# Hybrid attention layer on one core: the seven-product form in eight of the eleven down-projection blocks, the residual's turn in half parts, another order of the last additions

## The chip, the core and the metric

The kernel runs on one NeuronCore of a Trainium2 chip. Five engines work side by side, each through its own instructions in order: TensorE (PE: matmuls; PEld is its weight load), VectorE (DVE), ScalarE (ACT), GpSimd (POOL) and SyncE (SP), which here issues most DMAs. They wait for each other through semaphores. The metric is the device time of one execution in microseconds (us), the median of several runs; less is better. Before the change it is 385.23 us (three runs, 384.71 to 385.44).

## What is computed

One layer of a causal decoder on 256 tokens of width 1024, in float32: a norm, one input projection, two attention mixers with a gated merge, and then a gated feed-forward part with a short convolution, and a last norm. The change lies in the feed-forward part and the last norm:

```python
def conv_ffn(h, w_up, conv_w, conv_b, w_down):
    S = h.shape[1]
    u, gate = jnp.split(h @ w_up, 2, axis=-1)          # 2 x 2816 columns
    up = jnp.pad(u, ((0, 0), (CONV_WIDTH - 1, 0), (0, 0)))
    uc = conv_b
    for j in range(CONV_WIDTH):
        uc = uc + conv_w[j] * up[:, j:j + S]
    return (jax.nn.gelu(uc) * gate) @ w_down

# at the end of the layer
    x = x + conv_ffn(rmsnorm(x, g_ffn[l]), ...)
return rmsnorm(x, g_final)
```

## The kernel before

**Precision.** Every float32 operand of a large matmul is held as two parts, a high half (rounded to the PE's fast float32 form) and the rest (low half); a product is three matmuls: high x high, high x low, low x high. For each block of weights ACT writes the high half (`whi<-raw`, line 130) and DVE subtracts it from the raw weights (`wlo<-raw,whi`, line 134). Three buffers each exist for the raw weights, the high and the low halves. SP loads the raw weights, 1 MB a block (line 180), into a raw buffer whose split has ended.

**Units.** The kernel is a hand-written list of units, most with 1 MB of weights, and a loop over it (line 1211 on) that issues, for each unit, its matmuls, its evacuation, and the splits of the next units. The order of instructions on each engine is the order of that code. The feed-forward part has 11 blocks of 256 hidden columns. Block j has two units that multiply up (`mm_up`: first the convolved half, then the gate half, 48 matmuls of 128x256 each) and one that multiplies down, `downs[j]`, which stands two blocks later (`LAG` = 2).

**What DVE does for a block.** `ev_u` (lines 594 to 612) scales the first up-product out of PSUM (U), ACT and DVE make the convolution C, ACT its gelu; `ev_g` multiplies C with the second up-product (M); ACT copies M's high half (ah), and DVE writes its low half (al, line 642). Beside these stand the splits of the weights of later units, and in `turn` (line 1205) the turn of the residual: xT lies with the features in the partitions, and the end of the kernel needs X with the tokens there. DVE turns it in 32x256 pieces (STREAM_TRANSPOSE, line 1209), 32 in all, and after each of `downs[0]` to `downs[3]` stand eight of them.

**Eight or seven products.** A down-projection multiplies two halves of 128 hidden columns by 1024 output columns, for two groups of 128 tokens (t = 0, 1). The first 512 output columns (ch = 0) are done directly. For the other 512, `mm_down_part` makes eight products of 128x256, and `mm_sums` makes do with seven, after Strassen: it multiplies sums of the weights with sums of the activations and adds up in seven accumulators `ffn["P"]` in PSUM. With three matmuls a product a block has 48 matmuls directly and 24 + 21 = 45 with seven products. The sums cost work on DVE: `split_sums` makes sums of the weights (W, lines 171 to 173) and their halves (Wh on ACT, Wl on DVE, line 177), and `ev_g` three sums of M (lines 628 to 631), after which ah and al are 1024 wide and not 512. `split_sums` splits its block's weights two units ahead, and the direct blocks' are split one unit ahead. Blocks `FIRST_SUM` to 8 use seven products; before, FIRST_SUM is 4. The last two blocks (9 and 10) are direct.

**The end.** `downs[9]` and `downs[10]` are multiplied together, one output quarter after the other (`last`, line 1334), in the order (t, ch) = (0, 0), (0, 1), (1, 1), (1, 0). Ahead of it the results of the seven products are gathered: four subtractions into Q and five additions to X (`add`, line 1329). `last` adds a quarter to X, squares it (ACT), sums up the squares (POOL), multiplies with g_final into Y (POOL for the first tokens, DVE for the second), and `store` scales by the norm and writes the result. The quarters (0, 0) and (1, 1) lie in one PSUM tile (ps_s).

Of the kernel before, what the change touches and what calls it, by code (L numbers as in the profile page):

```python
# [15 lines left out]
OP = mybir.AluOpType  # L16
# [10 lines left out]
HALF = 1120  # L27
SHARED = {25: 1024, 26: 1024}
QUARTERS = ((0, 0, 512), (1, 0, 512), (0, 512, 256), (1, 512, 256), (1, 768, 256), (0, 768, 256))
FIRST_SUM = 4  # L30
EPS = 1e-6
BIG = 1e30
UW = 2240
# [62 lines left out]
def build(ctx, tc, a, out):  # L96
    nc = tc.nc
    V, A, P, T = nc.vector, nc.scalar, nc.gpsimd, nc.tensor
# [29 lines left out]
    def split_hi(u, c0=0, c1=None):  # L128
        c1 = c1 or u.n
        A.activation(u.hi[:, u.o + c0:u.o + c1], u.raw[:, c0:c1], AF.Copy)  # L130
# [9 lines left out]
    def hi_of(i):  # L140
        if 2 <= i < len(units):
            if units[i].load is not None:
                return
            split_tiles(units[i])
            split_hi(units[i], 0, 1792 if units[i] in downs[FIRST_SUM:NF - 2] else None)

    def lo_of(i):
        if 2 <= i < len(units):
# [7 lines left out]
            if i == NFIRST + 1:  # L156
                split_lo(units[i], 0, 1024)
                split_lo(units[i], 1024, 2048)
                return
            if units[i] in downs[FIRST_SUM:NF - 1]:  # L160
                return
# [431 lines left out]
    def ev_u(j):  # L593
        def f(u):
# [9 lines left out]

            if FIRST_SUM <= j - LAG:
                ffn.pop("sums")()
# [12 lines left out]
    def ev_g(j):  # L619
        def f(u):  # L620
# [4 lines left out]
            n = 4  # L625
            if FIRST_SUM <= j < NF - 2:
                n = 8
# [39 lines left out]
    def mm_sums(u, j):  # L667
# [4 lines left out]
        for q, x, k in ((2, 2, 1), (1, 0, 0), (3, 7, 2), (6, 6, 6), (5, 5, 4), (7, 4, 5), (4, 3, 7)):  # L672
            yh, yl = (wh[:, k], wl[:, k]) if k < 4 else (sh[:, k - 4], sl[:, k - 4])
            for n, (w, a_) in enumerate(((yh, h), (yh, l), (yl, h))):
                T.matmul(ffn["P"][q], a_[:, x], w, start=j == FIRST_SUM and n == 0 and q in (1, 5),  # L675
                         stop=j == NF - 3 and n == 2 and q in (1, 5, 6, 7), skip_group_check=True)
# [31 lines left out]
    downs = [Unit(2048, mm_down(j), o=48) for j in range(NF)]  # L708
# [452 lines left out]
    for n, f in zip(CHUNKS, first):  # L1161
        for c in range(0, 768 * n, 768):
            x, r = f[:, c:c + 256], [f[:, c + 256:c + 512], f[:, c + 512:c + 768]]
            if k == 0:
                r[1] = f[:, 520:776]
            h, h32, l = [[q[:, k * 256:k * 256 + 256] for q in t] for t in
                         ((u0.hi, u1.hi), (u0.hi.bitcast(F32), u1.hi.bitcast(F32)), (u0.lo, u1.lo))]
# [36 lines left out]

    def turn(n):

        b, t = n // 2, n % 2
        for j in range(4):
            V.transpose(X[32 * j:32 * j + 32, t].rearrange("p (k c) -> p k c", c=128)[:, :, 32 * b:32 * b + 32],  # L1209
                        xT[32 * b:32 * b + 32, :, t * 128 + 32 * j:t * 128 + 32 * j + 32])  # L1210

    post = []
    for i, u in enumerate(units):
        if i == FIRST_ITEM:
            rt["identr"] = att.tile([128, 128], F32R, name="identr")
            A.activation(rt["identr"], ident, AF.Copy)
        if i == 9:
            cmp_sum()
        for it in batches.get(i - 1, []):
            it.fin()  # L1220
        if i == FIRST_ITEM + 6:
            dil_tiles()
        for it in at(i):
            if isinstance(it, Dil):
                it.split()
        for it in at(i - 3):
            it.te()
        if i == 11:
            cmp_kv_ev()
        for it in at(i - 1):  # L1230
            it.sm()
        if i > 2 and i != 6:
            lo_of(i + 1)
        if i == 10:
            cmp_gelu()
        for it in at(i - 1):
            it.sm2()
        for it in at(i - 1):
            it.send("MA" if isinstance(it, Cmp) else {20: "KH", 21: "KL"}.get(i, "MB%d" % (i % 2)))
        load_to(i + LA)  # L1240
        if i == 14:
            nc.sync.dma_start(xT, a["xT"])
        if i == 3:
            hi_of(5)
            mixer_tiles()
            u1.evac(u1)
        if i == 4:
            split_keys()
        if i == 14:

            ob = att.tile([128, 4, S], F32R, name="ob", tag="qa")
            OB.update(h=ob[:, 0:2], l=ob[:, 2:4])
        if i in (23, 24):
            for c in range(2):
                m = ML[i - 23, c]
                A.activation(m, m, AF.Sigmoid)
        if i == NFIRST:
            st.close()
            ffn["pool"] = ctx.enter_context(tc.tile_pool(name="ffn", bufs=1))
            gf = ffn["pool"].tile([128, D], F32, name="gf")  # L1260
            nc.scalar.dma_start(gf, bass.AP(tensor=a["g_final"].tensor, offset=a["g_final"].offset,
                                            ap=[[0, 128], [1, D]]))
            X = ffn["pool"].tile([128, 2, D], F32, name="X")
            sq = ffn["pool"].tile([128, 512], F32, name="sq")
            Y = ffn["pool"].tile([128, 2, D], F32, name="Y")
        if 24 <= i <= 25:
            hi_of(i + 2)
        if i in (3, 24, NFIRST + 2):
            rt["kick"] = "own"
        u.mm(u)  # L1270
        if i == 2:
            split_tiles(units[3])
            for c in (0, 1024):
                split_hi(units[3], c, c + 1024)
        if not 24 <= i <= 26 and i > 1 and i != 3:
            hi_of(i + 2)
        if i == 5:
            lo_of(7)
        if units[min(i + 2, len(units) - 1)] in downs[FIRST_SUM:NF - 2]:
            split_sums(units[i + 2])  # L1280
        if units[min(i + 2, len(units) - 1)] is downs[NF - 2]:
            split_lo(units[i + 2])
        if i == 2:
            lo_of(3)
            row_scale()
            u0.evac(u0)
            ev_cmp2()
        if i == NFIRST + 1:
            rt["R2"] = rows_of(rt["rs2"], "R2", "o")
            units[NFIRST].evac(units[NFIRST])  # L1290
        if post:
            post.pop()()
        if u.pre:
            u.pre(u)
        if u.evac and i not in (0, 1, NFIRST):
            u.evac(u)
        if i == 4:
            tables_pool4()
        if i in (6, 7):
            q_parts(i - 6)  # L1300
        if i == 7:
            gates_of()
        if u in downs[:4]:
            for n in range(2):
                turn(2 * downs.index(u) + n)
        if u.pre:
            post.append(post_g(len([q for q in units[:i] if q.pre])))
        first = [it for it in at(i) if isinstance(it, Nsa) or isinstance(it, Dil) and it.t]
        for it in first:
            it.qk()  # L1310
        if i == 11:
            at(i)[-1].by_keys()
        for it in at(i - 2):
            it.tr()
        for it in at(i):
            if it not in first:
                it.qk()
        for it in batches.get(i, []):
            it.pv()
        if i == 9:  # L1320
            cmp_fold()
        if i == 10:
            cmp_kv()
# [4 lines left out]
    def add(xs, y, t):  # L1328
        V.scalar_tensor_tensor(xs, y, rt["rs2"][:, t:t + 1], xs, op0=OP.mult, op1=OP.add)

    def last(t, ch, c0=0, c1=512):

        xs, y = X[:, t, ch * 512 + c0:ch * 512 + c1], ffn["y"][t][ch][:, c0:c1]
        w = c1 - c0
        if c0:
            y = pd([512])[:, :w]
        for j in (NF - 2, NF - 1):
            mm_down_part(downs[j], j, [(t, ch)], c0, c1, y if c0 else None)
        n = {(0, 0): 0, (0, 1): 1, (1, 1): 2, (1, 0): 3}[t, ch] + (c0 > 0)
        ss, r = ss3[:, n:n + 1], rs3[:, t:t + 1]  # L1340
        add(xs, y, t)
        if c0:
            V.tensor_tensor_reduce(out=sq[:, w:2 * w], in0=xs, in1=xs, scale=1.0 / D, scalar=r,
                                   op0=OP.mult, op1=OP.add, accum_out=ss)
        else:
            A.activation(sq[:, :w], xs, AF.Square, scale=1.0 / 32, accum_out=ss)  # L1346
            P.tensor_tensor(out=r, in0=epsc if t == ch else r, in1=ss, op=OP.add)  # L1347
        if c0 or t < ch:
            P.tensor_tensor(out=r, in0=ss if c0 else r, in1=nhalf[:, 0:1], op=OP.pow)
        (V if t else P).tensor_tensor(out=Y[:, t, ch * 512 + c0:ch * 512 + c1], in0=xs,  # L1350
                                      in1=gf[:, ch * 512 + c0:ch * 512 + c1], op=OP.mult)

    def store(t, c):
# [8 lines left out]
    p, q = ffn["P"], ffn["pool"].tile([128, 4, 256], F32, name="Q", tag="W")  # L1362
    A.activation(q[:, 0], p[1], AF.Copy)
    add(X[:, 0, 512:768], p[1], 0)
    for o, l, r, op in ((1, p[6], q[:, 0], OP.subtract), (2, q[:, 1], p[5], OP.subtract),
                        (3, q[:, 2], p[7], OP.subtract), (0, p[7], q[:, 1], OP.subtract)):
        V.tensor_tensor(out=q[:, o], in0=l, in1=r, op=op)
    add(X[:, 0, 768:1024], q[:, 2], 0)
    add(X[:, 1, 768:1024], q[:, 3], 1)
    add(X[:, 1, 512:768], q[:, 0], 1)  # L1370
    add(X[:, 1, 256:512], ffn["y"][1][0][:, 256:512], 1)
    last(0, 0)
    last(0, 1)
    last(1, 1)
    last(1, 0, 0, 256)
# [23 lines left out]
```

## Time and profile before

| | |
|---|---|
| median of three runs | 385.23 us |
| the profiled execution | 385.59 us, of which its span is 383.8 us |
| granted TensorE clock | 0.999 of full speed |
| instructions in the trace | 8148 |
| the feed-forward part | from about 206 us on |
| PE's last matmul | ends at 377.7 us |
| DMA | 78.26 MB, 204 GB/s over the span |

The span is the time from the first to the last recorded instruction. The page gives the busy time of each engine; the view by stretches gives it for parts of the span; the view in order of time gives each instruction's start, its duration, its engine and line, what it writes and reads, and in brackets how long the engine had been idle before it and what ended that. PE's matmuls overlap, so the time that one of them takes in a row is longer than the distance to the next.

### The profile page before, as it was taken

How to read it: one execution, taken by the hardware profiler on the slowest of the kernel's cores; microseconds unless marked ns; L12 is line 12 of the kernel's file. 1: busy time of each engine (PE TensorE's matmuls, PEld its weight loads, DVE VectorE, ACT ScalarE, POOL GpSimd, SP SyncE). 2: the span in 40 equal slices, each digit the busy share in tenths (PEclk: the TensorE clock that was granted, in tenths of full speed). 3: DMA queues.
4: the chain of work that ended last, by engine and by line, in shares of the span. 5: the costliest groups of instructions: out<-in, count | busy, mean ns of one | idle time of the engine just before them, and what ended most of it. 6: DMA issues, size and time to landing. Idle time of an engine off the chain costs nothing.

```text
span 383.8 us, 8148 instructions
## 1 busy us (share of the span) xinstructions
PE 375.6 (98%) x3402; PEld 370.1 (96%) x3402; DVE 314.2 (82%) x543; ACT 221.7 (58%) x312; POOL 36.2 (9%) x63
## 2 busy tenths in 40 slices
PE   7999999999999999999999999999999999999993
PEld 6999999999999999999999999999999999999993
DVE  5969599994996876468887799798999999989774
ACT  4966536775985745745534765345462745755523
POOL 4021300001000000250333000000000000000013
PEclk9999999999999999999999999999999999999999
DMA  8999354468454656363547365365465475485002
GB/s 276 415 388 363 124 208 176 166 237 323 172 205 150 235 219 232 140 219 110 197 148 297 137 256 229 111 219 197 157 224 207 163 263 208 139 312 193 30 0 111
DMA packets 13717, 78.26 MB, mean 204 GB/s; under 512 B 1520, under 2 KB 2032, under 8 KB 6000
## 3 DMA queue, kind: packets, MB, share of 16 engines
q1 hardware_dynamic: 13248, 76.89, 54.4%
q10 hardware_dynamic: 432, 0.85, 0.6%
q8 instruction: 27, 0.44, 0.5%
q14 instruction: 10, 0.08, 0.1%
HBM read 71.05 MB, written 1.05 MB: 188 GB/s over the span
## 4 chain that ended last, share of the span: by engine, by line
PE 96%; DMA 2%; DVE 1%; ACT 0%; issue 0%; SPq 0%; POOLq 0%; POOL 0%; ACTq 0%
PE ps_d L205 36%; PE ps_d L210 18%; PE ps_s L661 6%; PE ps_t L661 5%; PE ps_o L205 5%; PE ps_d L308 3%; PE ps_o L210 3%; PE ps_d L365 2%; PE ps_t L205 2%; PE ps_o L675 2%; PE ps_t L908 2%; DMA first<-in_first_dram 2%; PE ps_o L977 1%; PE ps_o L563 1%; PE ps_o L1098 1%; PE ps_s L205 1%
## 5 line engine op out<-in xcount | busy, mean ns | idle before, releaser
L134 DVE TENSOR_TENSOR wlo<-raw,whi 128x2048 fp32r<-128x2048 f32 (+3 forms) x62 | 133.4, 2155 | 5.2 <-ACT whi L130 5.1
L130 ACT ACTIVATE whi<-raw 128x2048 fp32r<-128x2048 f32 (+3 forms) x62 | 113.7, 1839 | 10.7 <-DMA raw<-in_wts_dram 6.0
L205 PE MATMUL ps_d<-hTh,whi 128*128 128x256 f32 x512 | 119.0, 278 | 0.0
L205 PE MATMUL ps_d<-hTl,whi 128*128 128x256 f32 x512 | 117.9, 276 | 0.0
L205 PEld LDWEIGHTS ps_d<-hTh,whi 128*128 128x128 f32 x512 | 96.1, 188 | 0.9 <-issue 0.7
L205 PEld LDWEIGHTS ps_d<-hTl,whi 128*128 128x128 f32 x512 | 96.1, 188 | 0.0
L210 PE MATMUL ps_d<-hTh,wlo 128*128 128x256 f32 x512 | 63.3, 276 | 0.0
L210 PEld LDWEIGHTS ps_d<-hTh,wlo 128*128 128x128 f32 x512 | 60.5, 188 | 0.0
L602 ACT ACTIVATE C<-U,small 128x256 f32<-128x256 f32 x22 | 12.1, 595 | 27.1 <-DVE U L598 27.1
L610 DVE SCALAR_TENSOR_TENSOR C<-U,small,C 128x256 f32<-128x256 f32 x44 | 18.9, 479 | 4.1 <-ACT C L602 4.1
L633 ACT ACTIVATE ah<-M 128x512 fp32r<-128x512 f32 (+1 forms) x11 | 9.1, 829 | 22.6 <-DVE M L631 11.8
L945 ACT ACTIVATE E<-E,ast 128x256 f32<-128x256 f32 (+1 forms) x32 | 14.1, 450 | 9.6 <-DVE ast L940 7.7
L1347 POOL TENSOR_TENSOR tiny<-cst,tiny 128x1 f32<-128x1 f32 x2 | 0.5, 246 | 164.1 <-ACT sq L1346 164.1
L134 POOL TENSOR_TENSOR wlo<-raw,whi 128x1024 fp32r<-128x1024 f32 x3 | 7.8, 2600 | 71.3 <-ACT whi L130 71.3
L175 ACT ACTIVATE Wh<-W 128x1024 fp32r<-128x1024 f32 x5 | 5.3, 1065 | 15.8 <-DVE W L173 15.8
L1209 DVE STREAM_TRANSPOSE X<-xT 32x256 f32<-32x256 f32 x32 | 14.0, 436 | 0.4
L661 PE MATMUL ps_s<-whi,ah 128*128 128x256 f32 x68 | 11.8, 276 | 0.0
L661 PE MATMUL ps_s<-wlo,ah 128*128 128x256 f32 x68 | 11.8, 276 | 0.0
L661 PE MATMUL ps_s<-whi,al 128*128 128x256 f32 x68 | 11.8, 276 | 0.0
L205 PE MATMUL ps_d<-whi,hTh 128*128 128x256 f32 x48 | 11.3, 282 | 0.0
L623 DVE TENSOR_TENSOR M<-ps_d,C 128x512 f32<-128x512 f32 x10 | 6.9, 691 | 5.2 <-ACT C L616 3.0
L205 PE MATMUL ps_d<-whi,hTl 128*128 128x256 f32 x48 | 11.1, 277 | 0.0
(312 smaller groups left out, 773.7 us busy)
## 6 DMA issues: line engine op xcount, KB each, us to landing
raw<-in_wts_dram SPq DMA_DIRECT2D x59, 1024.0 KB, 4.8
Er<-E SPq DMA_DIRECT2D x6, 512.0 KB, 3.2
first<-in_first_dram SPq DMA_DIRECT2D x7, 384.0 KB, 7.2
Er<-E SPq DMA_DIRECT2D x6, 384.0 KB, 2.9
raw<-in_wts_dram SPq DMA_DIRECT2D x2, 560.0 KB, 9.3
xn<-in_xn_dram SPq DMA_DIRECT2D x2, 512.0 KB, 8.9
w1k<-in_wts_dram SPq DMA_DIRECT2D x2, 512.0 KB, 7.3
w1v<-in_wts_dram SPq DMA_DIRECT2D x2, 512.0 KB, 8.0
```

The source lines that it names most:

```text
L130: A.activation(u.hi[:, u.o + c0:u.o + c1], u.raw[:, c0:c1], AF.Copy)
L134: (eng or V).tensor_sub(u.lo[:, u.o + c0:u.o + c1], u.raw[:, c0:c1], u.hi.bitcast(F32)[:, u.o + c0:u.o + c1])
L205: T.matmul(po, l, r, start=start and bank not in banks, stop=False, skip_group_check=True)
L210: T.matmul(po, l, r, start=False, stop=stop and n == len(ks) - 1, skip_group_check=True)
L308: T.matmul(u.p[:, i], l[:, kt, i * 128:i * 128 + 128], r[:, kt], start=kt == 0 and i == 0 and q == 0, stop=kt == 7 and q == 2, skip_group_ ...
L365: T.matmul(u.p[:, i], l[:, kt, i * 128:i * 128 + 128], r[:, kt], start=kt == 0 and i == 0 and q == 0, stop=kt == 7 and q == 2, skip_group_ ...
L602: A.activation(C[:, c], U[:, c, 2:], AF.Identity, scale=CW(2, t), bias=CB[:, t:t + 1])
L610: V.scalar_tensor_tensor(C[:, c], U[:, c, w:w + S], CW(w, t), C[:, c], op0=OP.mult, op1=OP.add)
L633: A.activation(h[:, :n], M[:, :n], AF.Copy)
L661: T.matmul(ffn["y"][t][ch][:, b:b + 256] if own is None else own, x[:, 2 * kt + t], quarter(w, kt, ch, b), start=j == (0 if own is None el ...
L945: A.activation(self.E[:, i], self.E[:, i], AF.Exp, bias=mn[:, i:i + 1], scale=-1.0, accum_out=dn[:, i:i + 1])
L1209: V.transpose(X[32 * j:32 * j + 32, t].rearrange("p (k c) -> p k c", c=128)[:, :, 32 * b:32 * b + 32], xT[32 * b:32 * b + 32, :, t * 128 + ...
```

## The change

Three things change.

1. `FIRST_SUM` becomes 1: blocks 1 to 8 use seven products, and only blocks 0, 9 and 10 are direct.
2. `turn` does half a part (two pieces of 32x256), and `TURNS` lays the sixteen half parts after `downs[0]` to `downs[8]`: 4, 2, 2, 2, 2, 1, 1, 1, 1, which is 8, 4, 4, 4, 4, 2, 2, 2, 2 pieces. There are still 32 pieces.
3. At the end, `last(0, 0)` stands behind the first half of the gathering and not behind all of it, and the multiplication of (0, 1) with g_final moves from POOL to DVE.

```diff
-FIRST_SUM = 4
+FIRST_SUM = 1
+TURNS = (4, 2, 2, 2, 2, 1, 1, 1, 1)
...
     def turn(n):

-        b, t = n // 2, n % 2
-        for j in range(4):
+        b, t = n // 4, n % 4 // 2
+        for j in range(2 * (n % 2), 2 * (n % 2) + 2):
             V.transpose(X[32 * j:32 * j + 32, t].rearrange("p (k c) -> p k c", c=128)[:, :, 32 * b:32 * b + 32],
                         xT[32 * b:32 * b + 32, :, t * 128 + 32 * j:t * 128 + 32 * j + 32])
...
-        if u in downs[:4]:
-            for n in range(2):
-                turn(2 * downs.index(u) + n)
+        if u in downs[:len(TURNS)]:
+            n = downs.index(u)
+            for n in range(sum(TURNS[:n]), sum(TURNS[:n + 1])):
+                turn(n)
...
-        (V if t else P).tensor_tensor(out=Y[:, t, ch * 512 + c0:ch * 512 + c1], in0=xs,
+        (V if t or ch else P).tensor_tensor(out=Y[:, t, ch * 512 + c0:ch * 512 + c1], in0=xs,
                                       in1=gf[:, ch * 512 + c0:ch * 512 + c1], op=OP.mult)
...
     add(X[:, 0, 512:768], p[1], 0)
-    for o, l, r, op in ((1, p[6], q[:, 0], OP.subtract), (2, q[:, 1], p[5], OP.subtract),
-                        (3, q[:, 2], p[7], OP.subtract), (0, p[7], q[:, 1], OP.subtract)):
-        V.tensor_tensor(out=q[:, o], in0=l, in1=r, op=op)
+    V.tensor_sub(q[:, 1], p[6], q[:, 0])
+    V.tensor_sub(q[:, 2], q[:, 1], p[5])
     add(X[:, 0, 768:1024], q[:, 2], 0)
+    last(0, 0)
+    V.tensor_sub(q[:, 3], q[:, 2], p[7])
+    V.tensor_sub(q[:, 0], p[7], q[:, 1])
     add(X[:, 1, 768:1024], q[:, 3], 1)
     add(X[:, 1, 512:768], q[:, 0], 1)
     add(X[:, 1, 256:512], ffn["y"][1][0][:, 256:512], 1)
-    last(0, 0)
     last(0, 1)
```

What this does to DVE's order in a block is seen behind the turns that follow `downs[0]`. On DVE, before, from those turns (the first row) to the turns that follow `downs[1]`:

```order
L1209 STREAM_TRANSPOSE X<-xT 32x8x32 x8
L134 TENSOR_TENSOR wlo<-raw,whi 128x2048
L597 MEMSET U 128x2x2
L598 TENSOR_TENSOR U<-ps_d,R_2771 128x2x256
L610 SCALAR_TENSOR_TENSOR C<-U,small,C 128x256 x4
L134 TENSOR_TENSOR wlo<-raw,whi 128x2048
L623 TENSOR_TENSOR M<-ps_d,C 128x512
L134 TENSOR_TENSOR wlo<-raw,whi 128x2048
L642 TENSOR_TENSOR al<-M,ah 128x512
L1209 STREAM_TRANSPOSE X<-xT 32x8x32 x8
```

On DVE, after the change, from the same turns on (the rest of the block follows in the next piece):

```order
L1210 STREAM_TRANSPOSE X<-xT 32x8x32 x8
L135 TENSOR_TENSOR wlo<-raw,whi 128x2048
L172 TENSOR_TENSOR W<-raw 128x512
L173 TENSOR_TENSOR W<-W,raw 128x256
L174 TENSOR_TENSOR W<-W,raw 128x256
L135 TENSOR_TENSOR wlo<-raw,whi 128x1792
L598 MEMSET U 128x2x2
L599 TENSOR_TENSOR U<-ps_d,R_2771 128x2x256
L178 TENSOR_TENSOR Wl<-W,Wh 128x1024
L611 SCALAR_TENSOR_TENSOR C<-U,small,C 128x256 x4
```

The weights' sums and the split of `downs[1]` now stand ahead of U, and Wl behind it. The rest of that block on DVE, after the change:

```order
L624 TENSOR_TENSOR M<-ps_d,C 128x512
L629 TENSOR_TENSOR M<-M 128x256
L631 TENSOR_TENSOR M<-M 128x128
L632 TENSOR_TENSOR M<-M 128x128
L135 TENSOR_TENSOR wlo<-raw,whi 128x2048
L643 TENSOR_TENSOR al<-M,ah 128x1024
L1210 STREAM_TRANSPOSE X<-xT 32x8x32 x4
```

M has lost the split that stood between it and C, has got its three sums behind it, al is twice as wide, and half as many turns follow.

At the end of the kernel, on DVE, before, from the last split of weights to the addition of the quarter (0, 1) (ps_o, ps_t and ps_s are PSUM tiles; X<-ps_s is the quarter (0, 0)):

```order
L134 TENSOR_TENSOR wlo<-raw,whi 128x2048
L1329 SCALAR_TENSOR_TENSOR X<-ps_o,tiny,X 128x256
L1367 TENSOR_TENSOR Q<-ps_o,Q 128x256
L1367 TENSOR_TENSOR Q<-Q,ps_o 128x256 x2
L1367 TENSOR_TENSOR Q<-ps_o,Q 128x256
L1329 SCALAR_TENSOR_TENSOR X<-Q,tiny,X 128x256 x3
L1329 SCALAR_TENSOR_TENSOR X<-ps_t,tiny,X 128x256
L1329 SCALAR_TENSOR_TENSOR X<-ps_s,tiny,X 128x512
L1329 SCALAR_TENSOR_TENSOR X<-ps_t,tiny,X 128x512
```

The same place on DVE after the change:

```order
L1210 STREAM_TRANSPOSE X<-xT 32x8x32 x2
L135 TENSOR_TENSOR wlo<-raw,whi 128x2048
L1331 SCALAR_TENSOR_TENSOR X<-ps_o,tiny,X 128x256
L1367 TENSOR_TENSOR Q<-ps_o,Q 128x256
L1368 TENSOR_TENSOR Q<-Q,ps_o 128x256
L1331 SCALAR_TENSOR_TENSOR X<-Q,tiny,X 128x256
L1331 SCALAR_TENSOR_TENSOR X<-ps_s,tiny,X 128x512
L1371 TENSOR_TENSOR Q<-Q,ps_o 128x256
L1372 TENSOR_TENSOR Q<-ps_o,Q 128x256
L1331 SCALAR_TENSOR_TENSOR X<-Q,tiny,X 128x256 x2
L1331 SCALAR_TENSOR_TENSOR X<-ps_t,tiny,X 128x256
L1331 SCALAR_TENSOR_TENSOR X<-ps_t,tiny,X 128x512
```

Two turns stand ahead of the last split, and the addition X<-ps_s has moved ahead of two of the four subtractions and three of the additions.

## The prediction

> **What bounds the kernel now.** I read the page first, then the busy times by stretch, then VectorE's (DVE's) instructions in order of time. The page's busy shares and its chain of waits:
>
> ```profile
> PE 375.6 (98%) x3402; PEld 370.1 (96%) x3402; DVE 314.2 (82%) x543; ACT 221.7 (58%) x312; POOL 36.2 (9%) x63
> ...
> PE 96%; DMA 2%; DVE 1%; ACT 0%; issue 0%; SPq 0%; POOLq 0%; POOL 0%; ACTq 0%
> ```
>
> TensorE (PE) is the bound: the chain that ended last is 96% PE, and DVE has a fifth of the span free. But a share over the span says nothing of one stage. The feed-forward stage, by stretches (busy us of each engine, granted clock, DMA):
>
> ```profile
> 227.00:276.00 49.00, 49.00 (x435) 49.00 (x434) 43.04 (x61) 23.80 (x21) 0.00 (x0) 1.00 0.55 201
> ...
> 296.00:341.00 45.00, 45.00 (x400) 45.00 (x399) 42.16 (x57) 26.86 (x24) 0.00 (x0) 1.00 0.59 212
> ```
>
> The third number with a count is DVE. From 227 to 276 us (blocks with eight products) it is busy 43.04 of 49.00 us, 88%; from 296 to 341 us (blocks with seven) 42.16 of 45.00, 94%. PE is full in both. So a block with seven products fills DVE nearly as much as PE, and it does so in a stretch in which no turn of the residual stands. The change puts turns into exactly such blocks. What PE needs for one, from its own timeline (the low-half matmuls of an up-projection, one block apart, and the last block's):
>
> ```profile
> 306.29 1.98 PE L210 MATMUL ps_d<-hTh,wlo 128*128 128x256 f32 x16
> ...
> 322.27 1.98 PE L210 MATMUL ps_d<-hTh,wlo 128*128 128x256 f32 x16
> ...
> 368.85 0.62 PE L661 MATMUL ps_s<-wlo,ah 128*128 128x256 f32 x4
> ```
>
> Between the first two lie 48 + 48 + 45 = 141 matmuls in 15.98 us, 0.1133 us each. Nine matmuls fewer are 1.02 us.
>
> **What DVE needs for a block.** I count rounds, from one start of U<-ps_d (row L598) to the next. One round with eight turns and the step from eight to seven products, and one with seven products and no turns:
>
> ```profile
> 276.18 0.68 DVE L598 TENSOR_TENSOR U<-ps_d,R 128x512 f32<-128x512 f32 x1
> ...
> 281.52 0.69 DVE L623 TENSOR_TENSOR M<-ps_d,C 128x512 f32<-128x512 f32 x1
> ...
> 283.24 2.28 DVE L134 TENSOR_TENSOR wlo<-raw,whi 128x2048 fp32r<-128x2048 f32 x1
> 285.44 1.22 DVE L642 TENSOR_TENSOR al<-M,ah 128x1024 fp32r<-128x1024 f32 x1
> 286.67 3.61 DVE L1209 STREAM_TRANSPOSE X<-xT 32x256 f32<-32x256 f32 x8
> 290.31 2.29 DVE L134 TENSOR_TENSOR wlo<-raw,whi 128x2048 fp32r<-128x2048 f32 x1
> ...
> 295.99 0.68 DVE L598 TENSOR_TENSOR U<-ps_d,R 128x512 f32<-128x512 f32 x1
> ...
> 300.17 0.69 DVE L623 TENSOR_TENSOR M<-ps_d,C 128x512 f32<-128x512 f32 x1 [0.78 <-ACT C L616]
> ...
> 304.09 1.22 DVE L642 TENSOR_TENSOR al<-M,ah 128x1024 fp32r<-128x1024 f32 x1
> 305.23 2.28 DVE L134 TENSOR_TENSOR wlo<-raw,whi 128x2048 fp32r<-128x2048 f32 x1
> ...
> 310.90 0.68 DVE L598 TENSOR_TENSOR U<-ps_d,R 128x512 f32<-128x512 f32 x1
> ```
>
> - The round of the step takes 295.99 - 276.18 = 19.81 us, with no wait for PE in it.
> - A round of seven products without turns takes 310.90 - 295.99 = 14.91 us. The 0.78 us before M is inside: the split that used to stand there has moved away, so DVE waits for ScalarE's (ACT's) gelu. Against PE's 15.98 us DVE gains 1.07 us a round.
> - Turns: from al to the split behind them 290.31 - 285.44 = 4.87 us with eight, 305.23 - 304.09 = 1.14 us with none, so eight cost 3.73 us. Their busy time is 3.61 us, 0.45 each; I put the other 0.12 us down as fixed for a group. Groups of four and of two stand nowhere in the trace: four cost between 1.81 us (0.45 each, nothing fixed) and 2.28 (one more turn's time as the fixed part); I take 0.45 each + 0.12, 1.93 and 1.03 us, since it lies with the one group that the trace shows.
>
> So a round with four turns takes 14.91 + 1.93 = 16.84 us, **0.86 us more than PE needs**, and one with two 15.94 us, as long as PE's.
>
> **The sum.** The change makes blocks 1 to 3 (from 0) seven-product blocks and lays the turns as 8, 4, 4, 4, 4, 2, 2, 2, 2 behind blocks 0 to 8. I follow DVE from the first place that differs:
>
> ```profile
> 223.57 0.68 DVE L623 TENSOR_TENSOR M<-ps_o,C 128x512 f32<-128x512 f32 x1
> 224.17 2.27 DVE L134 TENSOR_TENSOR wlo<-raw,whi 128x2048 fp32r<-128x2048 f32 x1
> 226.37 0.68 DVE L642 TENSOR_TENSOR al<-M,ah 128x512 fp32r<-128x512 f32 x1
> ...
> 227.05 0.69 DVE L598 TENSOR_TENSOR U<-ps_d,R 128x512 f32<-128x512 f32 x1
> ...
> 243.37 0.69 DVE L598 TENSOR_TENSOR U<-ps_d,R 128x512 f32<-128x512 f32 x1 [1.49 <-PE ps_d L210]
> ```
>
> 1. Block 1's M gets its three sums: M to split 283.24 - 281.52 = 1.72 us in place of 224.17 - 223.57 = 0.60; al grows from 0.68 to 1.22. The next U moves from 227.05 to 227.05 + 1.12 + 0.54 = 228.71.
> 2. The round behind it is now the step, with eight turns: 228.71 + 19.81 = 248.52. Before, it ended at 243.37, and 1.49 us of it was waiting for PE; that wait is used up.
> 3. Four rounds with four turns: 4 x 16.84 = 67.36, to 315.88. Two with two turns: 31.88, to 347.76.
> 4. The last round, before:
>
> ```profile
> 340.70 0.68 DVE L598 TENSOR_TENSOR U<-ps_d,R 128x512 f32<-128x512 f32 x1
> ...
> 345.77 0.69 DVE L623 TENSOR_TENSOR M<-ps_d,C 128x512 f32<-128x512 f32 x1 [1.67 <-PE ps_d L210]
> ...
> 356.25 0.69 DVE L598 TENSOR_TENSOR U<-ps_d,R 128x512 f32<-128x512 f32 x1 [1.31 <-PE ps_d L210]
> ...
> 359.92 2.29 DVE L134 TENSOR_TENSOR wlo<-raw,whi 128x2048 fp32r<-128x2048 f32 x1 [0.26 <-ACT whi L130]
> ...
> 363.51 0.69 DVE L642 TENSOR_TENSOR al<-M,ah 128x512 fp32r<-128x512 f32 x1 [0.70 <-ACT ah L633]
> 365.32 2.29 DVE L134 TENSOR_TENSOR wlo<-raw,whi 128x2048 fp32r<-128x2048 f32 x1 [1.12 <-ACT whi L130]
> ```
>
> It took 15.55 us with two waits for PE: 1.31, and 1.67 of which 0.78 is the gelu and stays. Without them and with two turns: 15.55 - 1.31 - 0.89 + 1.03 = 14.38, to **362.14** in place of 356.25.
>
> 5. From that U to the end of the last split of weights (365.32 + 2.29 = 367.61) are 11.36 us, of splits and of hand-overs between DVE and ACT that all start from U. Block 8's two turns (0.93 us) fall into the 1.12 us wait in it; unhidden they would cost 0.93. The split now ends at 362.14 + 11.36 = 373.50. PE used it at 368.85, with 1.24 us in hand; now it starts some 0.03 us behind it, at 373.53: **4.68 us late**.
>
> PE's 1.02 us buys nothing here: it turns into new waits for DVE, some 0.9 us a block at the low-half matmuls of the first up-projection from about 290 us on, and over 2 us in the last two blocks. Behind such a wait on PE stand 16 matmuls, then the second up-projection's 48, whose result DVE's M needs: 64 x 0.1133 = 7.3 us after the split. DVE's next M comes 300.17 - (283.24 + 2.28) = 14.7 us after it, so DVE does not wait in turn, and the lateness does not feed on itself. ACT gets a copy (Wh) and a longer ah in each of the three blocks; in the stretch with seven products it is busy 26.86 of 45.00 us, so they lie beside DVE's work. SP's and ACT's issues of DMA keep their order.
>
> 6. The end. Rows of before (DVE, then PE's second tokens, DVE and POOL):
>
> ```profile
> 371.15 0.74 DVE L1329 SCALAR_TENSOR_TENSOR X<-ps_s,tiny,X 128x512 f32<-128x512 f32 x1
> ...
> 372.03 0.65 PE L661 MATMUL ps_s<-whi,ah 128*128 128x256 f32 x4
> ...
> 374.98 0.75 DVE L1329 SCALAR_TENSOR_TENSOR X<-ps_s,tiny,X 128x512 f32<-128x512 f32 x1 [2.00 <-PE ps_s L661]
> 375.03 1.30 POOL L1350 TENSOR_TENSOR Y<-X,gf 128x512 f32<-128x512 f32 x1
> ...
> 375.77 1.12 DVE L1350 TENSOR_TENSOR Y<-X,gf 128x512 f32<-128x512 f32 x1
> ...
> 378.02 0.19 POOL L1347 TENSOR_TENSOR tiny<-tiny 128x1 f32<-128x1 f32 x1 [1.09 <-ACT sq L1346]
> 378.33 0.48 DVE L1343 CUSTOM_DVE_ANT_0 sq<-X,tiny 128x256 f32<-128x256 f32 x1
> ```
>
> The addition of the first tokens (X<-ps_s) ended 371.89 - 367.61 = 4.28 us behind the last split; PE's second tokens write the same tile and come 372.03 - 368.85 = 3.2 us behind the split's use. In the old order a late split would cost another 1.1 us there. Drawn ahead of half of the gathering (two subtractions and three additions, some 1.9 us) it ends in time, so this part costs nothing and saves that 1.1. The product with gf that POOL gives up runs on DVE in the 2.00 us in which it waits for PE's next result; beside a gathering that is late by what the split is late, little of that wait is left, but a product of 0.7 to 1.1 us still ends about when that result comes. The other one, 1.12 us on DVE at 375.77, ran beside POOL's 1.30. The nearest row alone is the 128x512 sum in the same rounds:
>
> ```profile
> 292.52 0.69 DVE L171 TENSOR_TENSOR W<-raw 128x512 f32<-128x512 f32 x1
> ```
>
> If it falls to that, the square and POOL's sum behind it come 0.4 us sooner, and the last reduction starts at the end of the last addition, about 0.1 us earlier; otherwise nothing. I take 0.1. The Trainium skill, GPSIMD Engine Reference, section Specifications, says that GpSimd's SBUF interfaces are shared with VectorE and contend with DVE instructions with two SBUF inputs. By that rule the 0.1 us comes; without it, 0; the trace agrees so far as 1.12 beside 0.69 goes.
>
> Together 4.68 - 0.1 = **+4.6 us** against the profiled execution's 385.59 (span 383.8), 390.2. That execution lies 0.36 us above the median of 385.23; from the median it is **389.8**.
>
> **The rivals.**
> - *The work stays hidden, and PE sets the end* (the other side). Its place is DVE's idle time, 1.49 us in the first round and the like in the next, 0.89 + 1.31 in the last, and the 1.24 us at the end. The price is then -1.02 - 0.1: 384.5 profiled, **384.1**. For it: PE is full in both stretches, and DVE idles 18% of the span. It decides at the point where a round of DVE is shorter than 15.98 us; four turns in 14.91 go past that by 0.86. Only turns under 0.27 us each would bring it back. Chance 0.09. The Trainium skill, Perfetto Trace Analysis, section Identifying the Most-Contended Engine, tells one to take LDWEIGHTS busy as TensorE's measure and to improve the engine with the highest share first; by it (PEld 96%, DVE 82%) this rival is the forecast. The stretches agree on the order before the change, and do not on what is left over: 2.84 us of DVE in 45.
> - *The end catches up.* The hand-overs with ACT in step 5 (0.26 + 0.70 + 1.12 us idle on DVE) would be done already when DVE comes late. Against it: each starts from an instruction of DVE behind U. It gives 389.8 - 2.1 = **387.7**. Chance 0.12.
> - *Late splits make late loads.* A raw buffer is loaded anew when its split has ended:
>
> ```profile
> raw<-in_wts_dram SPq DMA_DIRECT2D x59, 1024.0 KB, 4.8
> ...
> raw<-in_wts_dram SPq DMA_DIRECT2D x2, 560.0 KB, 9.3
> ```
>
> A round of 16.8 us leaves room for 4.8, and for 9.3 still; three loads a round that hold each other up would bring that in. With 0.3 us in each of six rounds, **391.6**. Chance 0.07.
> - *Within 0.2%* by several small errors: 0.04.
>
> **How the numbers follow.** The forecast has 0.68. Its own bounds: no fixed part in the seven groups that count, -0.8; a whole turn's time in each, (0.45 - 0.12) x 7 = +2.3; block 8's turns unhidden, +0.9; the end without gain, +0.1. The upper ones are far from the nearest row, and I take them by half. The range takes in the second and third rival: **387.4 to 391.6**. A measurement of this kernel can tell 0.2% (0.8 us) from no change: faster 0.09, within 0.04, slower 0.87.
>
> **What would show it.** In the profile after, DVE is busy nearly all of 245 to 360 us; U<-ps_d comes every 16.8 us, then 15.9; its wait for PE before U is gone; PE has waits for wlo from 290 us on, and the largest near 370 us. Right rounds with a smaller delay mean that step 5 is wrong. If DVE still waits for PE at every U, the first rival holds. If the last addition comes over 9 us behind the last split, step 6 is wrong.

## The result, and the profile after

The changed kernel takes 389.46 us (median of 4 runs, 389.03 to 390.67) beside 385.15 us for the kernel before (4 runs, 384.71 to 385.44): 4.3 us more, a ratio of 1.0111 with a 95% interval of 1.0085 to 1.0137. The forecast was 389.8, in a range of 387.4 to 391.6. The profiled execution took 389.63 us, of which its span is 387.3. One of the five runs of e1 below, the profiled one, took 390.06 us and the other four 383.42 to 384.59, so e1's ratio goes by those four, and no times are read from its trace.

The page after, busy shares and the chain of waits:

```profile
PE 376.7 (97%) x3393; PEld 370.4 (96%) x3393; DVE 325.3 (84%) x565; ACT 224.9 (58%) x315; POOL 35.0 (9%) x62
...
PE 56%; DVE 28%; ACT 8%; issue 6%; DMA 1%; POOLq 0%; POOL 0%; ACTq 0%
```

The first line has hardly changed: PE has nine matmuls fewer (3393) and still the highest share, and DVE went from 82% to 84%. The second tells the story: the chain that ended last was 96% PE and is now 56% PE, 28% DVE and 8% ACT. The same by stretches, PE first, DVE third:

```profile
227.00:276.00 49.00, 49.00 (x433) 48.94 (x432) 45.95 (x67) 26.32 (x24) 0.00 (x0) 1.00 0.53 189
276.00:296.00 20.00, 19.44 (x169) 19.25 (x168) 18.89 (x27) 8.94 (x8) 0.00 (x0) 1.00 0.52 177
296.00:341.00 45.00, 44.45 (x387) 44.10 (x386) 42.04 (x60) 26.71 (x24) 0.00 (x0) 1.00 0.53 190
```

From 227 to 276 us DVE rose from 43.04 to 45.95 us busy, and PE is still full. From 296 to 341 us DVE is as busy as before (42.04 against 42.16), but PE now makes 387 matmuls where it made 400. So DVE is at its limit in both, but gets fewer blocks done now that turns lie in them, and PE goes at DVE's pace. The waits show it. PE's, and one of DVE's:

```profile
PE ps_s L662 <- DVE wlo L135: 1.1, 1, 1.1
PE ps_d L211 <- DVE wlo L135: 1.1, 2, 0.6
PE ps_s L662 <- ACT whi L131: 1.0, 1, 1.0
...
DVE M L624 <- ACT C L617: 6.1, 8, 0.8
```

PE waits for the split weights, in the middle of the stage (ps_d, the low halves of an up-projection) and at its end (ps_s). DVE no longer waits for PE before U. What is left of its idle time is above all ACT's gelu ahead of M, eight times some 0.77 us: between C and M the program has nothing else for DVE to do. DVE's rows in order of time, from block 1's M to the last split:

```profile
222.72 0.68 DVE L624 TENSOR_TENSOR M<-ps_o,C 128x512 f32<-128x512 f32 x1
...
227.77 0.68 DVE L599 TENSOR_TENSOR U<-ps_d,R 128x512 f32<-128x512 f32 x1
...
247.41 0.68 DVE L599 TENSOR_TENSOR U<-ps_d,R 128x512 f32<-128x512 f32 x1
...
255.52 1.22 DVE L643 TENSOR_TENSOR al<-M,ah 128x1024 fp32r<-128x1024 f32 x1
256.75 1.78 DVE L1210 STREAM_TRANSPOSE X<-xT 32x256 f32<-32x256 f32 x4
258.57 2.29 DVE L135 TENSOR_TENSOR wlo<-raw,whi 128x2048 fp32r<-128x2048 f32 x1
...
264.24 0.68 DVE L599 TENSOR_TENSOR U<-ps_d,R 128x512 f32<-128x512 f32 x1
...
314.71 0.68 DVE L599 TENSOR_TENSOR U<-ps_d,R 128x512 f32<-128x512 f32 x1
...
330.63 0.68 DVE L599 TENSOR_TENSOR U<-ps_d,R 128x512 f32<-128x512 f32 x1
...
346.56 0.68 DVE L599 TENSOR_TENSOR U<-ps_d,R 128x512 f32<-128x512 f32 x1
...
360.84 0.68 DVE L599 TENSOR_TENSOR U<-ps_d,R 128x512 f32<-128x512 f32 x1
...
369.90 2.29 DVE L135 TENSOR_TENSOR wlo<-raw,whi 128x2048 fp32r<-128x2048 f32 x1 [0.18 <-ACT whi L131]
```

The step takes 247.41 - 227.77 = 19.64 us, a round with four turns 264.24 - 247.41 = 16.83 (four of them to 314.71, 16.825 in the mean), the two with two turns 15.92 and 15.93, the last 14.28. Four turns lengthen the way from al to the split by 258.57 - 255.52 - 1.14 = 1.91 us. PE at the end of the stage, where the last weights are used:

```profile
369.92 0.74 PE L662 MATMUL ps_s<-whi,ah 128*128 128x256 f32 x4 [1.02 <-ACT whi L131]
...
372.25 0.72 PE L662 MATMUL ps_s<-wlo,ah 128*128 128x256 f32 x4 [1.14 <-DVE wlo L135]
372.81 0.39 PE L662 MATMUL ps_t<-whi,ah 128*128 128x256 f32 x2
```

The last split ends at 369.90 + 2.29 = 372.19, and PE uses it 0.06 us later. In the profile before it had 1.24 us in hand.

One thing must be known to compare the two traces: block 1's M, ahead of which the programs are the same in the feed-forward part, starts at 223.57 before and at 222.72 after. The execution that was profiled after was 0.85 us sooner there, which is taken for chance: two executions of one and the same kernel (e5 and e10 below) lie 0.56 us apart at that place, 222.66 and 223.22. So the span grew by only 3.5 us, where the medians differ by 4.3; measured from block 1's M, PE's use of the last split moved from 145.28 us (368.85 - 223.57) to 149.53 (372.25 - 222.72), **4.25 us**.

### The profile page after: what moved, and what is told of

Same layout as the page of the kernel before. It is cut to its first block, busy times and chain, and to the rows that moved or that the text cites. A ratio compares the mean times of both kernels' runs of the same rounds, so it can differ in the third digit from the quotient of the medians.

```text
span 387.3 us, 8155 instructions
## 1 busy us (share of the span) xinstructions
PE 376.7 (97%) x3393; PEld 370.4 (96%) x3393; DVE 325.3 (84%) x565; ACT 224.9 (58%) x315; POOL 35.0 (9%) x62
## 4 chain that ended last, share of the span: by engine, by line
PE 56%; DVE 28%; ACT 8%; issue 6%; DMA 1%; POOLq 0%; POOL 0%; ACTq 0%
PE ps_d L206 20%; DVE wlo L135 13%; PE ps_d L211 10%; ACT whi L131 4%; PE ps_o L206 3%; DVE X L1210 3%; PE ps_d L366 3%; PE ps_d L309 3%; DVE al L643 2%; DVE M L624 2%; PE ps_t L206 2%; DVE U L599 2%; ACT C L603 2%; PE ps_t L909 2%; PE ps_o L211 2%
## 5 line engine op out<-in xcount | busy, mean ns | idle before, releaser
L131 ACT ACTIVATE whi<-raw 128x2048 fp32r<-128x2048 f32 (+3 forms) x62 | 112.5, 1827 | 7.6 <-DMA raw<-in_wts_dram 3.7
L176 ACT ACTIVATE Wh<-W 128x1024 fp32r<-128x1024 f32 x8 | 8.5, 1064 | 34.6 <-DVE W L174 34.6
L634 ACT ACTIVATE ah<-M 128x1024 fp32r<-128x1024 f32 (+1 forms) x11 | 10.4, 946 | 21.1 <-DVE M L632 17.1
L643 DVE TENSOR_TENSOR al<-M,ah 128x1024 fp32r<-128x1024 f32 (+1 forms) x11 | 11.8, 1074 | 0.7 <-ACT ah L634 0.7
L206 PE MATMUL ps_o<-mixh,whi 128*128 128x256 f32 x48 | 11.0, 276 | 0.0
L206 PE MATMUL ps_o<-mixl,whi 128*128 128x256 f32 x48 | 11.0, 276 | 0.0
```

The lines of the kernel that those rows point to most:

```text
L206: T.matmul(po, l, r, start=start and bank not in banks, stop=False, skip_group_check=True)
L643: V.tensor_sub(l[:, :n], M, h.bitcast(F32)[:, :n])
```

## The experiments

The theory: a seven-product block fills DVE (14.91 us of PE's 15.98), each group of turns on top costs what it lasts, and the lateness adds up until the last split. Its rivals: the time comes from the seven products themselves, from late loads, or from the end. Each kernel is compared with the kernel before, measured beside it on the same chip (e1, e4, e5 and e6 on one, e2, e3 and e7 on a second, e8, e9 and e10 on a third):

| | edit | median us (runs) | ratio to before, 95% |
|---|---|---|---|
| e1 | change, without turns | 383.9 (5) | 0.9969, 0.9952 to 0.9986 |
| e2 | before, with the new turns and end | 385.1 (12) | 0.9997, 0.9988 to 1.0005 |
| e3 | before, with the new end | 385.18 (11) | 1.0003, 0.9995 to 1.0012 |
| e4 | change, with the old turns | 391.7 (4) | 1.0189, 1.0151 to 1.0226 |
| e5 | change, some turns in the gelu waits | 384.06 (8) | 0.9978, 0.9967 to 0.9989 |
| e6 | change, with the old end | 390.72 (4) | 1.015, 1.0133 to 1.0166 |
| e7 | e5 with the old end | 385.65 (12) | 1.0007, 0.9999 to 1.0016 |
| e10 | e5 once more | 383.99 (6) | 0.9962, 0.9947 to 0.9976 |
| e8 | e5 with the old order of the end | 385.24 (12) | 0.9998, 0.9988 to 1.0007 |
| e9 | e5 with eight products in blocks 1 to 3 | 384.86 (12) | 0.9989, 0.9979 to 1.0000 |

**e1: no turns.**

```diff
             X = ffn["pool"].tile([128, 2, D], F32, name="X")
+            nc.scalar.dma_start(X, a["xn"])
...
-            for n in range(sum(TURNS[:n]), sum(TURNS[:n + 1])):
-                turn(n)
+            pass
```

> The changed kernel without any turn of the residual; X is loaded as the untransformed x by one 1 MB DMA on ACT's queue instead, so the residual lacks what attention added to it. Theory (a VectorE round of 14.91 us plus its turns must fit into the 15.98 us that TensorE needs for a block): without turns every round fits, TensorE waits for nothing, and the nine matmuls come out in full: 385.15 - 1.0 = 384.1 us, and U<-ps_d every 15.98 us. Rival (the sums of weights and activations cost their 4 us a block themselves, by the hand-overs between DVE and ACT): the time stays at 388 us or more, and TensorE still waits for wlo.

383.9 us, the theory's 384.1 to within 0.2: without the turns the seven products are worth about 1 us (the interval says 0.5 to 1.8) and cost nothing. So the price is not that of the sums of weights, of ACT's copies or of the loads by themselves, all of which this kernel has. That U comes every 15.98 us, as expected, is not shown.

**e4: the old turns on seven-product blocks.**

```diff
-TURNS = (4, 2, 2, 2, 2, 1, 1, 1, 1)
+TURNS = (4, 4, 4, 4)
```

> The changed kernel with the turns where they were before, eight pieces after each of blocks 0 to 3. The sum of VectorE's work is the same. Theory (each round has to fit, and what TensorE has lost is not won back): three rounds of 14.91 + 3.73 = 18.64 us against 15.98; TensorE waits some 1.8 us at the first (the slack that is left there goes off) and 2.7 at each of the next two, nothing at the end; -1.0 + 7.2 = +6.2, 391.3 us. Rival (only VectorE's total counts, it is simply the busier engine): as the changed kernel, 389.5 us.

391.7 us, near the theory's 391.3 and over the rival's 389.5. PE's waits, then DVE's rows:

```profile
PE ps_d L211 <- DVE wlo L135: 4.9, 6, 1.4
```

```profile
248.13 0.68 DVE L599 TENSOR_TENSOR U<-ps_d,R 128x512 f32<-128x512 f32 x1
...
257.46 3.58 DVE L1210 STREAM_TRANSPOSE X<-xT 32x256 f32<-32x256 f32 x8
...
266.75 0.68 DVE L599 TENSOR_TENSOR U<-ps_d,R 128x512 f32<-128x512 f32 x1
...
304.00 0.69 DVE L599 TENSOR_TENSOR U<-ps_d,R 128x512 f32<-128x512 f32 x1
318.91 0.68 DVE L599 TENSOR_TENSOR U<-ps_d,R 128x512 f32<-128x512 f32 x1
```

A round with eight turns takes 266.75 - 248.13 = 18.62 us, 2.64 more than PE's 15.98; one without takes 14.91, as in the kernel before. The groups now measured are 3.71 us for eight (18.62 - 14.91), 1.92 for four, 1.02 for two: 0.45 a turn and 0.12 or 0.13 fixed. All of PE's waits lie in the up-projections, and none at the end, where DVE gains 1.07 us a round. That gain buys nothing back: PE has already lost its time, and then sets the pace itself. The same 32 turns cost more, the more unevenly they lie. PE's idle time in these six waits, 4.9 us, is less than the 7.2 expected. Each wait costs PE some 0.28 us more than its idle time shows (worked out for the changed kernel under step 5 below), which makes it 6.6.

**e6: the change with the old end.** The additions in the old order, and the product of (0, 1) on POOL.

```diff
-        (V if t or ch else P).tensor_tensor(out=Y[:, t, ch * 512 + c0:ch * 512 + c1], in0=xs,
+        (V if t else P).tensor_tensor(out=Y[:, t, ch * 512 + c0:ch * 512 + c1], in0=xs,
...
+    for o, l, r, op in ((1, p[6], q[:, 0], OP.subtract), (2, q[:, 1], p[5], OP.subtract),
+                        (3, q[:, 2], p[7], OP.subtract), (0, p[7], q[:, 1], OP.subtract)):
+        V.tensor_tensor(out=q[:, o], in0=l, in1=r, op=op)
     add(X[:, 0, 768:1024], q[:, 2], 0)
-    last(0, 0)
-    V.tensor_sub(q[:, 3], q[:, 2], p[7])
-    V.tensor_sub(q[:, 0], p[7], q[:, 1])
...
+    last(0, 0)
```

> The changed kernel with the old end: all of the gathering ahead of the quarter (0, 0), and the product of (0, 1) on POOL. Theory (the prediction's step 6): the last split of weights comes late, the addition of (0, 0) ends 4.3 us behind it, and TensorE's second tokens, which write the same PSUM tile, wait some 1.1 us for it: 390.6 us. Rival (that wait is not there, or something else ends later): 389.5 us.

390.72 us, 1.26 over the change's median, or 1.5 by the two ratios, since the two were not measured side by side. PE's waits have a new line, for the addition that frees the first tokens' PSUM:

```profile
PE ps_s L662 <- DVE X L1331: 0.7, 1, 0.7
```

**e2: the turns alone**, with FIRST_SUM back at 4 (the new end stays).

```diff
-FIRST_SUM = 1
+FIRST_SUM = 4
```

> FIRST_SUM is 4 again (blocks 0 to 3 with eight products); the turns as 4, 2, 2, 2, 2, 1, 1, 1, 1 half parts and the new order at the end stay. Theory: the loss of the change needs both edits, since only seven-product blocks are full. Here four pieces fall into one round of seven products (16.84 us against PE's 15.98, 0.86 us more), two pieces into the others (15.94, as long as PE's); the blocks of eight products have room, and the 2.1 us by which U waited for PE at block 5 of before, or what is left of it, covers the 0.86: 385.0 +- 0.4, no change, and no wait of PE for wlo above 0.3 us. Rival: the turns in full blocks alone cost what they add, 0.9 us and the stalls behind every split that is a few tenths late: 386 to 387.

385.1 us, no change. DVE's U rows around the step and the full blocks:

```profile
275.39 0.69 DVE L599 TENSOR_TENSOR U<-ps_d,R 128x512 f32<-128x512 f32 x1 [1.53 <-PE ps_d L211]
...
293.55 0.68 DVE L599 TENSOR_TENSOR U<-ps_d,R 128x512 f32<-128x512 f32 x1
...
310.37 0.68 DVE L599 TENSOR_TENSOR U<-ps_d,R 128x512 f32<-128x512 f32 x1
...
326.30 0.68 DVE L599 TENSOR_TENSOR U<-ps_d,R 128x512 f32<-128x512 f32 x1
```

The one round of seven products with four turns again takes 16.82 us and the next, with two, 15.93, yet PE does not wait for a split: DVE comes into them with time in hand, as its wait of 1.53 us for PE ahead of the step shows. So neither edit costs anything alone (e1: seven products without turns; e2: turns with few seven-product blocks). It takes both.

**e3: the end alone**, on the kernel before.

```diff
-        (V if t else P).tensor_tensor(out=Y[:, t, ch * 512 + c0:ch * 512 + c1], in0=xs,
+        (V if t or ch else P).tensor_tensor(out=Y[:, t, ch * 512 + c0:ch * 512 + c1], in0=xs,
...
-    for o, l, r, op in ((1, p[6], q[:, 0], OP.subtract), (2, q[:, 1], p[5], OP.subtract),
-                        (3, q[:, 2], p[7], OP.subtract), (0, p[7], q[:, 1], OP.subtract)):
-        V.tensor_tensor(out=q[:, o], in0=l, in1=r, op=op)
     add(X[:, 0, 768:1024], q[:, 2], 0)
+    last(0, 0)
...
-    last(0, 0)
```

(with the four subtractions as in the change)

> The kernel before with the new end alone: the addition of the quarter (0, 0) ahead of half of the gathering, and the product of (0, 1) with g_final on VectorE and not on GpSimd. Theory: before, VectorE's last split was 1.1 us and more ahead of PE, so no buffer was late and the order is worth nothing; the product of the second tokens falls from 1.12 to 0.69 us, but the last addition waits for PE's last product anyway: 385.0, 0 to -0.1. Rival: the product that is 0.43 us shorter shows at the end: 384.6.

385.18 us beside 385.2: nothing.

**e5 and e10: some turns in the wait for the gelu.** DVE waits 0.77 us for ACT ahead of M in every seven-product block, and two pieces take 0.9. Seven groups of two move there, 14 of the 32 pieces; the rest stay behind the blocks.

```diff
-TURNS = (4, 2, 2, 2, 2, 1, 1, 1, 1)
+TURNS = (4, 1, 1, 1, 0, 0, 0, 1, 1)
+GAP = {3: (9,), 4: (10,), 5: (11,), 6: (12,), 7: (13,), 8: (14,), 9: (15,)}
...
             M = f_.tile([128, 8, 128], F32, name="M", tag="M", bufs=2)
+            for n in GAP.get(j, ()):
+                ffn["turn"](n)
...
+    ffn["turn"] = turn
     post = []
```

> The changed kernel with the same 32 pieces at other places: two pieces directly ahead of M in blocks 3 to 9, where VectorE stands still 0.78 us for ACT's gelu, and the rest after the blocks as 8, 2, 2, 2, 0, 0, 0, 2, 2. Theory: two pieces (0.9 us) nearly fill the 0.78, a round with two of these and two after the block is 14.91 + 0.2 + 1.03 = 16.1 us and one without the latter 15.1; TensorE waits under 0.6 us in all: 384.1 to 384.7 us. Rival (a piece costs 0.45 us wherever it stands): VectorE's total is unchanged, 389.5 us.

> The kernel of e5 once more, beside the two that follow, so that the three are compared on the same chip. Theory: the seven-product form saves PE 9 x 0.1133 = 1.02 us and no split is late: 1.0 us under the kernel before. Rival: what e5 gained was partly the chip it ran on: 0.3 us or less.

384.06 us, and 383.99 on another chip: 1.0 and 1.3 us under the kernel before, both intervals below 1, and in neither trace does PE wait for a split. It does the same work as the change. By stretches, and a round on DVE (e10):

```profile
296.00:341.00 45.00, 45.00 (x400) 45.00 (x399) 44.26 (x61) 26.87 (x24) 0.00 (x0) 1.00 0.58 209
```

```profile
280.10 0.68 DVE L600 TENSOR_TENSOR U<-ps_d,R 128x512 f32<-128x512 f32 x1
...
283.53 0.89 DVE L1213 STREAM_TRANSPOSE X<-xT 32x256 f32<-32x256 f32 x2
284.45 0.69 DVE L627 TENSOR_TENSOR M<-ps_d,C 128x512 f32<-128x512 f32 x1
...
289.61 0.88 DVE L1213 STREAM_TRANSPOSE X<-xT 32x256 f32<-32x256 f32 x2
...
296.20 0.68 DVE L600 TENSOR_TENSOR U<-ps_d,R 128x512 f32<-128x512 f32 x1
```

The round carries four turns, as in the change, and takes 16.10 us, not 16.83: the two ahead of M took the place of the idle time, and no wait stands there. DVE is busy 44.26 of 45.00 us, PE is full, and its 400 matmuls are back.

**e7 and e8: does the order at the end still matter there?** Both are e5 with the first addition behind the whole gathering again, as in the diff of e6; e7 also gives the product of (0, 1) back to POOL.

> The kernel with two pieces of the turn directly ahead of M in blocks 3 to 9 (384.06 us) with the order of the end as it was before the change, and the product of (0, 1) on GpSimd again. Theory: its last split ends only 0.2 us ahead of PE's use (366.79 against 367.01 us), and the addition that frees PSUM for the second tokens stands 4.28 us behind the split in the old order, at 370.98 us, where PE wants the buffer at 370.19: PE waits 0.8 us there, 384.9. Rival: the order at the end costs only where the last split is late, and here it isn't: 384.1.

> The kernel of e5 with the addition of the quarter (0, 0) behind the whole gathering again; the product of (0, 1) stays on VectorE. Theory: the order alone makes the wait of PE that e7 showed (the PSUM buffer comes free about 0.9 us late, and the second matmul after a wait is 0.1 us late too): 1.0 us over the kernel of e5 on this chip. Rival: the product beside GpSimd (1.11 us against 0.69) has a part in it: 0.6 us over or less.

385.65 us (e7) and 385.24 (e8, 1.25 over e10 on the same chip). e7 and e5 ran on different chips; by their ratios e7 is 1.1 us over e5, where 0.8 was expected. Their two traces can't be compared straight: the last split ends 0.8 us later in e7's, but block 1's M, ahead of which the programs are the same, already starts that much later (223.46 against 222.66). So the order's price is read from e8. The last split, the addition and PE's use of the tile in e10 (first three rows) and in e8:

```profile
364.97 2.29 DVE L136 TENSOR_TENSOR wlo<-raw,whi 128x2048 fp32r<-128x2048 f32 x1 [0.20 <-ACT whi L132]
...
368.95 0.75 DVE L1335 SCALAR_TENSOR_TENSOR X<-ps_s,tiny,X 128x512 f32<-128x512 f32 x1
...
370.66 0.62 PE L665 MATMUL ps_s<-whi,ah 128*128 128x256 f32 x4
```

```profile
364.20 2.29 DVE L136 TENSOR_TENSOR wlo<-raw,whi 128x2048 fp32r<-128x2048 f32 x1 [0.21 <-ACT whi L132]
...
370.03 0.74 DVE L1335 SCALAR_TENSOR_TENSOR X<-ps_s,tiny,X 128x512 f32<-128x512 f32 x1
...
370.83 0.74 PE L665 MATMUL ps_s<-whi,ah 128*128 128x256 f32 x4 [0.77 <-DVE X L1335]
```

In the new order the addition ends 0.96 us ahead of PE's use; in the old one it ends 4.28 us behind the split, as in the kernel before, and PE waits for it. The order alone does that. From one group of four matmuls to the next, PE takes 0.94 us more at this wait than e10 does there (by their starts, 369.44 to 370.83 against 370.21 to 370.66) and 0.12 more in the group behind it, 1.06 of the 1.25 us; the rest is not placed. e3 and e8 together: a reordering that is worth nothing beside a split with 1.2 us in hand is worth 1.25 us beside one with 0.2.

**e9: e5 with eight products in blocks 1 to 3** (FIRST_SUM = 4, as in e2's diff).

> The kernel of e5 with FIRST_SUM = 4 (blocks 0 to 3 with eight products); turns in the waits for the gelu and the new end stay. Theory: PE was the bound before and kept its 3402 matmuls here, so that where the turns stand is worth nothing: as the kernel before, within 0.3 us, and 1.0 us over the kernel of e5. Rival: the turns' place, not the nine matmuls, made e5's gain: 1.0 us under the kernel before.

384.86 us: by the ratios 0.4 us under the kernel before, with an interval that ends at no difference, and 0.9 over e10. So most of e5's gain is the nine matmuls (1.02 us of PE's time); whether the turns' place has a few tenths of its own stays open.

## Why the prediction held, point by point

The mechanism is the one forecast; the sizes, from block 1's M on (223.57 before, 222.72 after):

| step | predicted | measured |
|---|---|---|
| 1, block 1's M to the next U | 5.14 | 5.05 |
| 2, the step with eight turns | 19.81 | 19.64 |
| 3, four rounds with four turns | 67.36 | 67.30 |
| 3, two rounds with two | 31.88 | 31.85 |
| 4, the last round | 14.38 | 14.28 |
| 5, U to the end of the last split | 11.36 | 11.35 |
| 5, PE's use of that split, later by | 4.68 | 4.25 |
| 6, gain at the end | 0.1 | none seen |

- **Steps 1 to 4** were each 0.03 to 0.17 us too long, 0.45 together; the step between eight and seven products has most of it. The price of a group of turns, for which the trace before had only one of eight, was the term least sure, and held: 1.91 for four against 1.93.
- **Step 5** held to 0.01 us, and the rival that the end catches up (387.7) falls with it. The hand-overs do start from DVE, as ACT's rows show:

```profile
367.43 0.63 ACT L634 ACTIVATE ah<-M 128x512 fp32r<-128x512 f32 x1 [2.44 <-DVE M L624]
367.97 1.90 ACT L131 ACTIVATE whi<-raw 128x2048 fp32r<-128x2048 f32 x1
```

  ACT stands idle for 2.44 us until DVE's M is there, and the high half that PE waits for at 369.92 stands behind that copy of M in ACT's order. The two waits of the last blocks cost 1.02 and 1.14 us, "over 2 us" as forecast. The waits in the middle were put at 0.9 us a block; PE did fall behind by 16.83 - 15.98 = 0.85 a round. It shows as two idle times only, 0.56 us at 289.31 and 0.55 at 322.94, and each costs more than it shows: the matmul at 322.94 starts 0.83 us behind the one ahead of it (322.11), where 0.11 is usual, and the next one 0.22 us behind that, 0.72 + 0.11 = 0.83 together. In the round between the two PE fell behind not by waiting but by a slower pace (the last section).
- **Step 6**, first half: in the old order the split's lateness would cost "another 1.1"; e6 took 1.26 to 1.5 more, with PE's new wait in its trace, and e8 shows the order alone to do it. The half that failed is "I take 0.1". DVE's last rows after:

```profile
373.88 0.75 DVE L1331 SCALAR_TENSOR_TENSOR X<-ps_s,tiny,X 128x512 f32<-128x512 f32 x1
...
379.23 0.69 DVE L1352 TENSOR_TENSOR Y<-X,gf 128x512 f32<-128x512 f32 x1
...
381.17 0.48 DVE L1331 SCALAR_TENSOR_TENSOR X<-ps_d,tiny,X 128x256 f32<-128x256 f32 x1 [0.39 <-PE ps_d L662]
381.80 0.48 DVE L1345 CUSTOM_DVE_ANT_0 sq<-X,tiny 128x256 f32<-128x256 f32 x1
```

  The product did fall from 1.12 to 0.69 us, but DVE then waits 0.39 us for PE's last result, and the reduction starts 0.15 us after the last addition's end, with nothing left between them that a shorter product could take away. e3, with the same shorter product, is at 385.18 beside 385.2. The Trainium skill, GPSIMD Engine Reference, section Specifications, by which the product falls when GpSimd stands aside, agrees with the trace (1.12 and 0.69 us; 1.09 us in e6 and 1.11 in e7, where GpSimd multiplies beside it); it is only the time that it does not move. The sign named for this step, a last addition over 9 us behind the last split, does not decide it: the addition starts 8.98 us behind the split's end at 372.19 and ends 9.46 behind it.
- **The sum.** 4.25 us of lateness and 0.1 us in the matmuls behind PE's last wait (the four of 372.25 take 0.56 us, not 0.45) are 4.35, against 4.31 between the medians. The forecast's 4.6 was too much by the 0.43 of lateness, and too little by those 0.1 and by the gain of step 6 that did not come; that the total lies within 0.3 us owes something to these errors having opposite signs.
- **The other side.** "The work stays hidden, and PE sets the end" had the price of 384.1 and the right point of decision: it is what happened as soon as the turns went (e1, 383.9) or found idle time in the round (e5, 384.06). The Trainium skill, Perfetto Trace Analysis, section Identifying the Most-Contended Engine, by whose shares this rival was the forecast, asks for the engine with the highest share; over the whole span the shares after are nearly as they were before (PEld 96%, DVE 84%) although the kernel is 1.1% slower, and the measurement decides for the count by rounds. The next section of that page, Optimization Strategy, says that a kernel can have several regimes with different engines in front. By shares no stretch of the feed-forward shown here has one: even from 296 to 341 us after the change PE (44.45 us) and its weight load (44.10) stay above DVE (42.04). It is the waits that change sides.
- **Late loads** (391.6). ACT's high halves are the first to use a load. Their waits for one in the blocks from 228 to 368 us, after and before:

```profile
ACT whi L131 <- DMA raw<-in_wts_dram: 0.3, 1, 0.3
```

```profile
ACT whi L130 <- DMA raw<-in_wts_dram: 4.2, 4, 1.7
```

  There is less of it than before: the loads have longer rounds, and no stall on them feeds the lateness.

## What to carry to other kernels

Where one engine sets the pace, the room for another engine's extra work is counted per round, as the bound engine's period less the other's work and its unavoidable waits: here 15.98 - 14.91 = 1.07 us, in which two turns fit and four do not, though DVE idled a fifth of the span. Lateness from rounds that are too full adds up and is not given back by later rounds, so filler belongs evenly spread, and first of all into waits that the round has anyway: with all 32 pieces ahead of splits the kernel lost 4.3 us, and with 14 of them moved ahead of a product that waits for the gelu it gained 1. An order at the end can be worth nothing or a microsecond according to how late its input comes, so it is judged together with what makes that input late.

## What the runs showed of the hardware that was not expected

TensorE has two paces at the same granted clock. Two rounds of PE in the profile after, each from a low-half matmul that waited for its split (the clock is the 1.00 behind the counts):

```profile
289.31:306.11 16.80, 16.80 (x141) 16.66 (x141) 15.78 (x23) 8.92 (x9) 0.00 (x0) 1.00 0.54 189
...
322.94:338.90 15.96, 15.96 (x140) 15.96 (x141) 14.95 (x21) 8.97 (x9) 0.00 (x0) 1.00 0.56 198
```

The first makes 141 matmuls in 16.80 us, 0.119 each, the second 140 in 15.96, 0.114, both without a gap of PE. The slow round follows right on a wait of 0.56 us for a split, but another wait of nearly the same length, at 322.94, is followed by the fast pace. In e6's trace it is the other way round: behind a wait of 0.56 us at 289.52 PE keeps the fast pace, and behind one as long at 306.34 it makes 137 matmuls in 16.16 us, 0.118 each, at a clock of 1.00. So the wait alone does not decide it; what does is open. It cost nothing in the profile after, since DVE set the pace there: between 227 and 378 us DVE waits for PE nowhere.
